# Where the written order of an MLP's instructions begins and ends, in a two-layer attention kernel on one core

## The chip, the core and the metric

The kernel runs on one core of a Trainium2 chip. Its engines are TensorE (PE in the profile, with PEld for its weight loads), VectorE (DVE), ScalarE (ACT), GpSimd (POOL) and SyncE (SP, which here only issues DMAs). The metric is device microseconds (us) of one execution; before the change the median of three runs is 2160.49 us (2158.95 to 2161.11).

## The reference

Two layers on 256 tokens of width 2048, all in float32. Layer 0 is stick-breaking attention with 16 heads, layer 1 a native sparse attention (compressed, selected and windowed branches with gates); after each comes an MLP. What matters here is the skeleton:

```
def sqrelu_mlp(h, w1, w2):
    return jnp.square(jax.nn.relu(h @ w1)) @ w2

for layer in range(2):
    h = h + attention(rms_norm(h, norm_g))
    h = h + sqrelu_mlp(rms_norm(h, mlp_norm_g[layer]), mlp_w1[layer], mlp_w2[layer])
```

w1 is 2048 x 8192, w2 is 8192 x 2048.

## The kernel before

**Chunks.** Every large product is done in chunks of a 2 x 128-row by 512-column block (512 KB) of weights. SP loads a chunk into a `raw` tile (five in rotation; in the MLPs three loads in eight go into `more`, three in rotation). ScalarE rounds it to `hi` (L143) and VectorE makes the rest `lo = raw - hi` (L145); both have four buffers in rotation. TensorE then multiplies high and low halves in three products. A tile in rotation is free again when its last reader is done: the `hi` buffer of a chunk, when the chunk's `hi` matmuls have ended.

**What lies between two large products.** The activations are kept transposed, in `xs` (high and low). When a 512-column block of h is complete (`add_h`, L387, or L385 without a factor), `next_x` takes its square sums on ScalarE (`ssq`, L350, tile `junk`), TensorE transposes it (`make_x`, L329, four transposes into a bank of `att`), and ScalarE (L334) and VectorE (L336) write `xs`. The generator `next_x` is put into a list, and `pump`, called twice in each chunk, lets it advance.

**The MLP.** w1 is taken in four quarters of hidden columns (`fg`), each in four parts of eight chunks (`T` chunks, `chunk1`, L207). Of w2's products some output blocks are done plainly (`N` chunks, `chunk2`, L174) and some with Strassen's scheme (`S` chunks, `chunk7`, L270), whose sums `add_S` adds to h (`sum7`: first `uv` on ScalarE, L294, then seven steps on VectorE, L295 to L299); `sum2` adds a plain block. In the last quarter the order is 24 `N` chunks for output blocks 0, 1 and 3, eight `S` chunks for block 2 among them, and behind the last `S` chunk six more `N` chunks. `done` starts `next_x` for a block (first MLP) or stores it (second).

**What sets the order.** Each engine runs its instructions in the order in which they stand in the program. In general a scheduler sets that order when the program is built. Inside `tc.manual_schedule(engines=...)` the instructions of the named engines keep the order in which the kernel's code issues them. In the kernel before, all steps of an MLP are inside such a block, for TensorE, VectorE, ScalarE and SP: from the first chunk of w1 on, with the `next_x` of the last output block that `pump` mixes in, to the end, where the first MLP's `next_x` for the next attention is mixed in likewise. `plan()` yields the steps; `put(after, j, ...)` places a step behind the j-th chunk of a list.

Of the kernel before, what the change touches and what calls it, by code (L numbers as in the profile page):

```python
# [16 lines left out]
T = 256  # L17
# [18 lines left out]
SK = 2 * ST + NCMP  # L36
GATES = 3 * NH
JUNK = 1
SLOPES = [2.0 ** (-8.0 * (i + 1) / NH) for i in range(NH)]


@with_exitstack
def hybrid_kernel(
# [15 lines left out]
    att = ctx.enter_context(tc.tile_pool(name="att", bufs=4, space=PSUM))  # L59
# [358 lines left out]
    def mlp(l, layer, junk, done, last=None):  # L418
        w1, w2 = mlp_w1[l], mlp_w2[l]
        ss = far(junk, KD * 4 * P, "ss").rearrange("p (a k i n) -> p a k i n", a=2, k=KD // 2, i=4)  # L420
        factor = junk.tile([P, 64], F32, name="factor", bufs=1)[:, :NT]
        NK, NF, NG, KB = KD // KC, D // NB, DFF // D, NB // P
        banks, part = {}, {}

        def factors():
            yield
            r = make_rstd(layer)
            nc.vector.tensor_tensor(factor, r, r, op=OP.mult)

        def chunk1(fg, fb, i):  # L430
            if i == 0:
                banks["T", fb] = [bank(acc, "acc") for _ in range(KB // 2)]
            chunk_T(banks["T", fb], w1, i * KC, fg * D + fb * NB, i == 0, i == NK - 1)

        def relu(fb):
            a = part["s", fb] = junk.tile([P, KB, T], F32, tag="sq", name="sq", bufs=1)
            for j in range(0, KB, 2):
                nc.scalar.activation(
                    a[:, j:j + 2, :], banks["T", fb][j // 2].rearrange("p (m t) -> p m t", m=2), AF.Relu
                )  # L440

        def square(fb):
            s = part["s", fb]
            nc.scalar.activation(s, s, AF.Square)

        def high(fb):
            k, s = fb * KB, part["s", fb]
            nc.scalar.activation(yhi[:, k:k + KB, :], s, AF.Copy)
            sv = s.rearrange("p (j kk) t -> p j kk t", kk=2)
            a1, a2 = [[sv[:, :, kk, t * P:(t + 1) * P] for kk in (1, 0)] for t in range(NT)]  # L450
            q = part["q", fb] = junk.tile([P, 2, 4, P], F32, tag="sums", name="sums", bufs=1)
            nc.vector.scalar_tensor_tensor(q[:, :, 0, :], a2[0], -1.0, a2[1], op0=OP.mult, op1=OP.subtract)
            nc.vector.tensor_tensor(q[:, :, 2, :], a1[0], a2[0], op=OP.subtract)
            nc.vector.tensor_tensor(q[:, :, 1, :], a2[1], q[:, :, 2, :], op=OP.subtract)
            nc.vector.tensor_tensor(q[:, :, 3, :], a1[1], q[:, :, 1, :], op=OP.subtract)

        def low(fb):
            k, s = fb * KB, part["s", fb]
            nc.scalar.activation(ss[:, 0, k // 2:k // 2 + 2], part["q", fb], AF.Copy)
            nc.vector.tensor_tensor(ylo[:, k:k + KB, :], s, yhi[:, k:k + KB, :].bitcast(F32), op=OP.subtract)  # L460

        def low7(fb):
            k = fb * KB
            o = ss[:, :, k // 2:k // 2 + 2]
            nc.vector.tensor_tensor(o[:, 1], part["q", fb], o[:, 0].bitcast(F32), op=OP.subtract)

        def chunk2(fg, nb, i, first, end, turn, by_token=False):
            if first:
                banks["N", nb] = [bank(acc, "acc") for _ in range(NT)]
            chunk_N(banks["N", nb], w2, fg * KD + i * KC, nb * NB, first, end, yhi, ylo, koff=fg * KD,  # L470
                    by_token=by_token, turn=turn)

        def chunk7(fg, nb, i, first, end):
            if first:
                banks["S", nb] = banks_S(att, "att")
            chunk_S(banks["S", nb][1], w2, fg * KD + i * KC, nb * NB, first, end, yhi, ylo, ss[:, 0], ss[:, 1],
                    koff=fg * KD)

        def sum2(nb):
            add_h(nb, banks["N", nb], factor)  # L480

        def sum7(nb):
            add_S(nb, *banks["S", nb], junk, factor)

        def plan():


            def merge(plain, after):
                for j, c in enumerate(plain):
                    yield c  # L490
                    yield from after.pop(j, ())
                assert not after

            def do(f, *args):
                return lambda: f(*args)

            def Ts(fg, fb):
                return [("T", fg, fb, i) for i in range(NK)]

            def Ns(fg, nb, ks=range(NK)):  # L500
                return [("N", fg, nb, i, i == ks[0], i == ks[-1]) for i in ks]

            def Ss(fg, nb, at, after, ks=range(NK)):
                for i, j in zip(ks, at):
                    after.setdefault(j, []).append(("S", fg, nb, i, i == ks[0], i == ks[-1]))

            def put(after, j, *fs):
                after.setdefault(j, []).extend(fs)

            def stages(after, j, fb, stash=False):  # L510
                if not stash:
                    put(after, j, do(relu, fb))
                put(after, j, do(square, fb))
                for i, f in enumerate((high, low, low7)):
                    put(after, j + 1 + i, do(f, fb))

            half = NK // 2
            for fg in range(NG):
                after = {}
                if fg == 0:  # L520
                    plain = sum([Ts(0, fb) for fb in range(NF)], [])
                    for fb in range(NF - 1):
                        stages(after, fb * NK + NK + 2, fb)
                else:
                    plain = sum([Ts(fg, fb) for fb in range(1, NF)], [])
                    put(after, 2, do(sum7, 2))
                    put(after, 3, do(sum2, 1))
                    Ss(fg - 1, 3, (3, 5, 7, 10, 13, 15, 18, 21), after)
                    stages(after, 8, 0, True)
                    stages(after, 13, 1)  # L530
                    stages(after, 18, 2)
                yield from merge(plain, after)
                after = {}
                if fg:
                    put(after, 1, do(sum7, 3))
                stages(after, 2, NF - 1)
                if fg < NG - 1:
                    plain = Ns(fg, 0) + Ts(fg + 1, 0) + Ns(fg, 1, range(half, NK))
                    Ss(fg, 1, (4, 5, 6, 7), after, range(half))
                    put(after, 10, do(sum7, 1))  # L540
                    put(after, 11, do(sum2, 0))
                    Ss(fg, 2, (12, 13, 14, 15, 16, 17, 18, 19), after)
                    put(after, 18, do(relu, 0))
                else:
                    plain = Ns(fg, 0) + Ns(fg, 1) + Ns(fg, 3)
                    put(after, 10, do(sum2, 0))
                    Ss(fg, 2, (4, 6, 8, 10, 11, 13, 15, 17), after)
                    put(after, 17, do(sum2, 1))
                    put(after, 18, do(sum7, 2), *[do(done, n, (att, "att")) for n in range(3)])
                    if last is None:  # L550
                        put(after, 23, do(sum2, 3), do(done, 3, (att, "att")))
                yield from merge(plain, after)

        spawn(factors(), 1)
        with tc.manual_schedule(engines={mybir.EngineType.PE, mybir.EngineType.DVE, mybir.EngineType.Activation,
                                         mybir.EngineType.SP}):
            steps = list(plan())
            for n, c in enumerate(steps):
                if callable(c):
                    c()  # L560
                    continue
                follower = next((d[0] for d in steps[n + 1:] if not callable(d)), None)
                if c[0] == "T":
                    chunk1(*c[1:])
                elif c[0] == "S":
                    chunk7(*c[1:])
                elif last is not None and c[1:3] == (NG - 1, 3):
                    fg, nb, i, first, end = c[1:]
                    chunk2(fg, nb, i, first, i == NK - 2, False, end)
                else:  # L570
                    chunk2(*c[1:], turn=follower in ("T", "S"))
            if last is not None:
                add_out(3, banks["N", 3], last, factor)

# [627 lines left out]
```

## Time and profile before

| | |
|---|---|
| median of three runs | 2160.49 us |
| the profiled execution's own time | 2155.24 us |
| its span, first to last instruction | 2153.5 us |
| mean granted TensorE clock | 0.998 |
| TensorE busy | 2134.2 us (99%) |
| VectorE, ScalarE, GpSimd busy | 1654.2, 1232.2, 45.5 us |
| DMA | 406.38 MB, mean 189 GB/s |

The page gives the busy time of each engine; a view of waits tells for whom an engine waited; the timeline lists the instructions of one engine in order of time (start, duration, engine, line, operation, tiles, count, and in brackets the idle time before it and who ended it). A view by windows gives for each stretch of time its length, the busy time of an engine, and the clock that TensorE was granted. On TensorE the first MLP goes from 391.8 to 1080.5 us of the span, the second from 1465.0 us to the end.

### The profile page before, as it was taken

The page shows a single profiled execution, that of the slowest core. Times are in us where ns is not written, and L with a number is a line of the kernel's source. Part 1 is how long each engine was busy: PE and PEld are TensorE (multiplying, and loading weights), DVE is VectorE, ACT ScalarE, POOL GpSimd, SP SyncE. Part 2 cuts the span into 40 slices and gives each one's busy share as a digit, 9 for nine tenths or more (in the row PEclk, how much of TensorE's full clock was granted, in tenths as well). Part 3 has the DMA queues.
Part 4 walks back from the last instruction along what each step waited for, and adds up shares of the span by engine and source line. Part 5 has one row for each costly group of instructions (what it writes and reads, how often), then busy time and mean ns, then how long its engine had stood idle before and what let it go on. Part 6 is the DMA issues. An engine that isn't in the chain of part 4 may idle for free. (4 is left out here: it accounts for less than half of the span.)

```text
span 2153.5 us, 37647 instructions
## 1 busy us (share of the span) xinstructions
PE 2134.2 (99%) x15110; PEld 1979.8 (92%) x15110; DVE 1654.2 (77%) x2269; ACT 1232.2 (57%) x1683; POOL 45.5 (2%) x78
## 2 busy tenths in 40 slices
PE   9999999999999999999999999999999999999999
PEld 9999988899999999999898888888999999999997
DVE  5556556468989989889687888764589889899896
ACT  6555665455565565565455666654555655655653
POOL 0000000000000000000000100000000000000000
PEclk9999999999999999999999999999999999999999
DMA  7655555566766666666477554455657666666663
GB/s 238 211 169 176 160 182 178 184 202 184 213 196 200 201 205 196 197 214 199 144 197 219 168 145 137 147 189 157 203 185 213 196 200 205 203 197 198 208 214 118
DMA packets 260407, 406.38 MB, mean 189 GB/s; under 512 B 13188, under 2 KB 91912, under 8 KB 260232
## 3 DMA queue, kind: packets, MB, share of 16 engines
q1 hardware_dynamic: 258984, 401.95, 60.6%
q8 instruction: 118, 1.93, 0.4%
q0 software_dynamic: 432, 1.57, 0.2%
q10 hardware_dynamic: 816, 0.46, 0.1%
q14 instruction: 57, 0.47, 0.1%
HBM read 401.83 MB, written 2.10 MB: 188 GB/s over the span
## 5 line engine op out<-in xcount | busy, mean ns | idle before, releaser
L145 DVE TENSOR_TENSOR lo<-raw,hi 128x1024 fp32r<-128x1024 f32 x486 | 590.1, 1221 | 210.8 <-ACT hi L143 201.5
L143 ACT ACTIVATE hi<-raw 128x1024 fp32r<-128x1024 f32 x486 | 509.8, 1054 | 291.5 <-PE acc L174 122.4
L207 PE MATMUL acc<-xs,hi 128*128 128x256 f32 x5360 | 667.3, 277 | 8.3 <-ACT hi L143 7.7
L207 PEld LDWEIGHTS acc<-xs,hi 128*128 128x128 f32 x5360 | 635.9, 188 | 10.2 <-ACT hi L143 8.8
L207 PE MATMUL acc<-xs,lo 128*128 128x256 f32 x2680 | 361.4, 278 | 0.0
L207 PEld LDWEIGHTS acc<-xs,lo 128*128 128x128 f32 x2680 | 331.4, 189 | 0.0
L174 PE MATMUL acc<-hi,yhi 128*128 128x512 f32 x732 | 287.1, 392 | 2.9 <-ACT hi L143 2.9
L174 PE MATMUL acc<-hi,ylo 128*128 128x512 f32 x732 | 285.6, 390 | 0.0
L143 ACT ACTIVATE hi<-ts 128x1024 fp32r<-128x1024 f32 x136 | 144.3, 1061 | 186.8 <-DVE ts L250 185.3
L174 PE MATMUL acc<-lo,yhi 128*128 128x512 f32 x732 | 198.5, 392 | 1.1 <-DVE lo L145 1.1
L145 DVE TENSOR_TENSOR lo<-more,hi 128x1024 fp32r<-128x1024 f32 x129 | 157.4, 1220 | 45.9 <-ACT hi L143 45.2
L145 DVE TENSOR_TENSOR lo<-ts,hi 128x1024 fp32r<-128x1024 f32 x136 | 166.4, 1223 | 23.9 <-ACT hi L143 22.8
L174 PE MATMUL acc<-hi,xs 128*128 128x512 f32 x704 | 177.8, 392 | 0.0
L174 PEld LDWEIGHTS acc<-hi,yhi 128*128 128x128 f32 x732 | 137.4, 188 | 29.4 <-ACT hi L143 3.3
L174 PEld LDWEIGHTS acc<-lo,yhi 128*128 128x128 f32 x732 | 136.5, 188 | 29.8 <-DVE lo L145 2.0
L174 PEld LDWEIGHTS acc<-hi,ylo 128*128 128x128 f32 x732 | 137.5, 188 | 26.0 <-DVE ylo L316 0.2
L143 ACT ACTIVATE hi<-more 128x1024 fp32r<-128x1024 f32 x129 | 135.7, 1052 | 36.3 <-PE acc L207 21.1
L174 PEld LDWEIGHTS acc<-hi,xs 128*128 128x128 f32 x704 | 130.1, 188 | 26.0
L248 ACT ACTIVATE shi<-raw 128x768 fp32r<-128x768 f32 x73 | 61.8, 846 | 103.3 <-PE att L270 103.3
L270 PE MATMUL att<-hi,ss 128*128 128x256 f32 x816 | 114.6, 276 | 0.0
L248 ACT ACTIVATE shi<-more 128x768 fp32r<-128x768 f32 x63 | 53.2, 844 | 97.0 <-PE att L270 97.0
L270 PEld LDWEIGHTS att<-hi,ss 128*128 128x128 f32 x816 | 102.6, 188 | 0.0
(256 smaller groups left out, 2627.5 us busy)
## 6 DMA issues: line engine op xcount, KB each, us to landing
raw<-in_mlp_w_dram SPq DMA_DIRECT2D x320, 512.0 KB, 4.1
more<-in_mlp_w_dram SPq DMA_DIRECT2D x192, 512.0 KB, 4.1
raw<-in_sb_w_qkv_dram SPq DMA_DIRECT2D x95, 512.0 KB, 4.1
raw<-in_nsa_w_in_dram SPq DMA_DIRECT2D x50, 512.0 KB, 3.9
raw<-in_sb_w_out_dram SPq DMA_DIRECT2D x32, 512.0 KB, 4.2
raw<-in_nsa_w_in_dram SPq DMA_DIRECT2D x64, 256.0 KB, 3.8
raw<-in_nsa_w_out_dram SPq DMA_DIRECT2D x32, 512.0 KB, 3.6
w1t<-in_nsa_cmp_w_dram SPq DMA_DIRECT2D x8, 512.0 KB, 4.2
```

Of the source, the lines that this page charges most:

```text
L143: nc.scalar.activation(hi, raw, AF.Copy)
L145: nc.vector.tensor_tensor(lo, raw, hi.bitcast(F32), op=OP.subtract)
L174: mm = lambda a, b, k, t, s, e: nc.tensor.matmul(ps[t], a[:, k, t * P:(t + 1) * P], b, start=s, stop=e)
L207: nc.tensor.matmul(o, w, x[:, k0 + kk, :], start=s, stop=e, skip_group_check=True)
L248: nc.scalar.activation(hi, flat[:, :3 * W], AF.Copy)
L270: nc.tensor.matmul(ps[i], a, w, start=s, stop=e, skip_group_check=True)
```

## The change

The block of the written order no longer holds the whole MLP. It is entered at step `("T", 0, 1, 0)`, the first chunk of the second part of w1's first quarter; the eight chunks before it are left to the scheduler. In the first MLP it is closed behind the last `S` chunk by a marker in the plan (`FREE`); what follows (the sums, the six last `N` chunks, the `next_x` of the next attention) is left to the scheduler. In the second MLP it holds to the end, but `sum2(1)` moves from behind chunk 17 to behind chunk 18, and `sum7(2)` with three `done` from 18 to 20.

```diff
+FREE = "the scheduler's order from here"
...
                     Ss(fg, 2, (4, 6, 8, 10, 11, 13, 15, 17), after)
-                    put(after, 17, do(sum2, 1))
-                    put(after, 18, do(sum7, 2), *[do(done, n, (att, "att")) for n in range(3)])
                     if last is None:
+                        put(after, 17, FREE, do(sum2, 1), do(sum7, 2), *[do(done, n, (att, "att")) for n in range(3)])
                         put(after, 23, do(sum2, 3), do(done, 3, (att, "att")))
+                    else:
+                        put(after, 18, do(sum2, 1))
+                        put(after, 20, do(sum7, 2), *[do(done, n, (att, "att")) for n in range(3)])
...
-        with tc.manual_schedule(engines={mybir.EngineType.PE, mybir.EngineType.DVE, mybir.EngineType.Activation,
-                                         mybir.EngineType.SP}):
-            steps = list(plan())
+        steps = list(plan())
+        with ExitStack() as order:
             for n, c in enumerate(steps):
-                if callable(c):
+                if c == ("T", 0, 1, 0):
+                    order.enter_context(tc.manual_schedule(engines={
+                        mybir.EngineType.PE, mybir.EngineType.DVE, mybir.EngineType.Activation, mybir.EngineType.SP
+                    }))
+                if c == FREE:
+                    order.close()
+                elif callable(c):
                     c()
...
```

What this makes of the program's order, at three places. The changed file is eight lines longer; its line 144 is line 143 of the kernel before.

ScalarE at the start of the first MLP, before. `hi_3921` is the split of the first chunk of w1; `junk` are the square sums of h; `hi_3994`, `hi_4099` and `hi_4159` are splits out of `more`:

```order
L143 ACTIVATE hi_3921<-raw_3919 128x1024
L350 ACTIVATE junk_3949,ssq_3520<-h_77 128x512
L350 ACTIVATE junk_3951,ssq_3520<-h_77 128x512
L143 ACTIVATE hi_3955<-raw_3953 128x1024
L334 ACTIVATE xs_78<-att_3983,gT_90 128x256 x2
L143 ACTIVATE hi_3994<-more_3992 128x1024
L334 ACTIVATE xs_78<-att_4022,gT_90 128x256 x2
L143 ACTIVATE hi_4033<-raw_4031 128x1024
```

The same place with the change (`hi_3919` is now the split of the first chunk):

```order
L144 ACTIVATE hi_3919<-raw_3917 128x1024
L144 ACTIVATE hi_3953<-raw_3951 128x1024
L144 ACTIVATE hi_3992<-more_3990 128x1024
L144 ACTIVATE hi_4031<-raw_4029 128x1024
L351 ACTIVATE junk_3947,ssq_3520<-h_77 128x512
L351 ACTIVATE junk_3949,ssq_3520<-h_77 128x512
L144 ACTIVATE hi_4061<-raw_4059 128x1024
L144 ACTIVATE hi_4097<-more_4095 128x1024
L335 ACTIVATE xs_78<-att_3981,gT_90 128x256 x2
L144 ACTIVATE hi_4127<-raw_4125 128x1024
L335 ACTIVATE xs_78<-att_4020,gT_90 128x256 x2
```

Three splits moved ahead of the square sums, and two more ahead of the first `xs`; the start of the second MLP moves in the same way. On TensorE nothing moves at these two places. On SP, the loads there with the change:

```order
L159 DMA raw<-in_sb_w_out_dram 128x2x512 x19
L159 DMA more<-in_mlp_w_dram 128x2x512
L159 DMA raw<-in_sb_w_out_dram 128x2x512
L159 DMA more<-in_mlp_w_dram 128x2x512
L159 DMA raw<-in_sb_w_out_dram 128x2x512
L159 DMA more<-in_mlp_w_dram 128x2x512
L159 DMA raw<-in_sb_w_out_dram 128x2x512 x11
L159 DMA raw<-in_mlp_w_dram 128x2x512 x7
```

Before, all 32 loads of the output projection's weights stood ahead of the MLP's first; now three loads into `more` stand ahead of 13, 12 and 11 of them.

ScalarE at the end of the first MLP, before, from the split of the last `S` chunk (`hi_11505`) on; `hi_11534` is the split of the first `N` chunk behind it, `uv` the first step of the Strassen sum:

```order
L143 ACTIVATE hi_11505<-ts_11497 128x1024
L143 ACTIVATE hi_11534<-more_11532 128x1024
L294 ACTIVATE uv_11550<-att_11005 128x256
L143 ACTIVATE hi_11561<-raw_11559 128x1024
L350 ACTIVATE junk_11578,ssq_11577<-h_77 128x512
L350 ACTIVATE junk_11580,ssq_11577<-h_77 128x512
L143 ACTIVATE hi_11584<-raw_11582 128x1024
L334 ACTIVATE xs_78<-att_11596,gT_90 128x256 x2
L334 ACTIVATE xs_78<-att_11609,gT_90 128x256 x2
L143 ACTIVATE hi_11620<-more_11618 128x1024
```

With the change:

```order
L144 ACTIVATE hi_11505<-ts_11497 128x1024
L144 ACTIVATE hi_11544<-more_11542 128x1024
L351 ACTIVATE junk_11619,ssq_11560<-h_77 128x512
L351 ACTIVATE junk_11621,ssq_11560<-h_77 128x512
L144 ACTIVATE hi_11567<-raw_11565 128x1024
L144 ACTIVATE hi_11603<-raw_11601 128x1024
L144 ACTIVATE hi_11625<-more_11623 128x1024
L295 ACTIVATE uv_11533<-att_11005 128x256
L144 ACTIVATE hi_11661<-raw_11659 128x1024
L351 ACTIVATE junk_11677,ssq_11560<-h_77 128x512
L144 ACTIVATE hi_11683<-more_11681 128x1024
L335 ACTIVATE xs_78<-att_11579,gT_90 128x256 x2
```

Square sums and three splits moved ahead of `uv`, two more splits ahead of the first `xs`. TensorE's transposes of this stretch stand one `N` chunk earlier, the last of them one chunk of the next projection earlier.

VectorE at the end of the second MLP, with the change (before, `lo_23370` and `lo_23388` stood, under other numbers, behind the last of the `h<-uv` additions, and the two `h<-acc` one row earlier):

```order
L146 TENSOR_TENSOR lo_23350<-raw_23346,hi_23348 128x1024
L388 SCALAR_TENSOR_TENSOR h_77<-acc_22950,factor_15730,h_77 128x512
L388 SCALAR_TENSOR_TENSOR h_77<-acc_22951,factor_15730,h_77 128x512
L146 TENSOR_TENSOR lo_23370<-more_23366,hi_23368 128x1024
L146 TENSOR_TENSOR lo_23388<-raw_23384,hi_23386 128x1024
L296 TENSOR_TENSOR uv_23402<-att_22824,uv_23402 128x256
L297 TENSOR_TENSOR uv_23402<-att_22823,uv_23402 128x256
```

The `lo` halves of two `N` chunks moved ahead of the Strassen sum.

More of the change, by code (lines that the diff above doesn't have):

```diff
@@ L552, in plan @@
                 yield from merge(plain, after)
         spawn(factors(), 1)
-        with tc.manual_schedule(engines={mybir.EngineType.PE, mybir.EngineType.DVE, mybir.EngineType.Activation,
-                                         mybir.EngineType.SP}):
-            steps = list(plan())
+        steps = list(plan())
+        with ExitStack() as order:
             for n, c in enumerate(steps):
-                if callable(c):
-                    c()
[L561 to L569, printed above, removed]
-                else:
-                    chunk2(*c[1:], turn=follower in ("T", "S"))
+                if c == ("T", 0, 1, 0):
[5 more added lines that the diff above has]
+                elif callable(c):
+                    c()
+                else:
+                    follower = next((d[0] for d in steps[n + 1:] if not callable(d) and d != FREE), None)
+                    if c[0] == "T":
+                        chunk1(*c[1:])
+                    elif c[0] == "S":
+                        chunk7(*c[1:])
+                    elif last is not None and c[1:3] == (NG - 1, 3):
+                        fg, nb, i, first, end = c[1:]
+                        chunk2(fg, nb, i, first, i == NK - 2, False, end)
+                    else:
+                        chunk2(*c[1:], turn=follower in ("T", "S"))
```

## The prediction

> **What bounds the kernel now.** The page's first part has TensorE busy for 2134.2 us of a span of 2153.5 us, so no edit off TensorE pays unless TensorE waits for it. I read next who TensorE waits for (line, releaser, total us, times, longest), over the whole span:
>
> ```profile
> PE acc L207 <- ACT hi L143: 7.7, 5, 1.9
> PE acc L174 <- ACT hi L143: 2.9, 2, 1.9
> PE acc L174 <- DVE lo L145: 1.1, 2, 0.6
> PE acc L207 <- ACT xs L334: 0.6, 1, 0.6
> ```
>
> The busy total hides more than these 12.3 us: a matmul at half clock counts as busy. So I cut the stretches where the waits lie (columns: from:to, length, TensorE busy and instructions, granted clock, share of the DMA engines, GB/s). The first, third and fifth are the start of the first MLP, its end with the seam to the next attention, and the start of the second MLP; the last is the end of the second MLP; the second and fourth are undisturbed pieces for comparison.
>
> ```profile
> 391.77:409.71 17.94, 14.19 (x105) 0.91 0.33 89
> 409.71:420.64 10.93, 10.93 (x97) 1.00 0.87 286
> 1057.04:1096.30 39.26, 35.24 (x229) 1.00 0.46 137
> 1465.02:1484.83 19.81, 15.87 (x106) 0.83 0.30 81
> 1484.83:1495.79 10.96, 10.96 (x97) 0.99 0.88 287
> 2134.98:2138.56 3.58, 3.00 (x13) 1.00 0.18 71
> ```
>
> What a chunk (24 matmuls of 256 columns, or 12 of 512) should take is read from the timeline of TensorE: from one chunk's start to the next 2.72 us (412.48 to 415.20; 380.60 to 383.32), and 3.20 us where a group of four transposes (L329) stands between (374.57 to 377.77), so 0.48 us a group.
>
> ```profile
> 374.57 0.48 PE L174 MATMUL acc<-hi,yhi 128*128 128x512 f32 x1
> 377.77 0.48 PE L174 MATMUL acc<-hi,yhi 128*128 128x512 f32 x1
> 380.60 0.39 PE L174 MATMUL acc<-hi,yhi 128*128 128x512 f32 x1
> 383.32 0.39 PE L174 MATMUL acc<-hi,yhi 128*128 128x512 f32 x1
> 412.48 1.98 PE L207 MATMUL acc<-xs,hi 128*128 128x256 f32 x16
> 415.20 1.98 PE L207 MATMUL acc<-xs,hi 128*128 128x256 f32 x16
> ```
>
> **Why TensorE waits at the start of an MLP.** ScalarE's timeline there:
>
> ```profile
> 382.61 1.06 ACT L143 ACTIVATE hi<-raw 128x1024 fp32r<-128x1024 f32 x1 [1.66 <-PE acc L174]
> 392.17 0.63 ACT L350 ACTIVATE junk<-h 128x512 f32<-128x512 f32 x1 [8.50 <-DVE h L385]
> 398.14 0.84 ACT L334 ACTIVATE xs<-att,gT 128x256 fp32r<-128x256 f32 x2 [3.54 <-PE att L329]
> 398.87 1.05 ACT L143 ACTIVATE hi<-more 128x1024 fp32r<-128x1024 f32 x1
> 403.46 0.84 ACT L334 ACTIVATE xs<-att,gT 128x256 fp32r<-128x256 f32 x2 [3.54 <-PE att L329]
> ```
>
> ScalarE works in order. The split of chunk 0 runs at 382.61; the next row in its queue is the square sum of h, which waits 8.50 us for the last addition to h; the split of chunk 2 (`hi<-more`) stands behind `xs`, which waits for transposes that TensorE does behind chunk 1. Nothing holds the split itself: its tile was filled long before, and its `hi` buffer (four in rotation) comes free with the last but one chunk of the output projection. So TensorE transposes, then idles 1.87 us for `xs` and the split behind it, twice (3.7 of the 7.7 us above). At 1465 the same happens, with 0.19 + 1.87 + 1.87 us.
>
> **The change there.** Outside the written order, ScalarE splits chunks 1, 2 and 3 ahead of the square sums, and 4 and 5 ahead of the first `xs`. TensorE's own order stays; only its input comes earlier. I walk it: the `hi` buffers come free as the last output chunks end their `hi` half, one each 2.72 us, so splits 1 to 3 run at about 385.4, 388.1 and 390.8 and are done before chunk 0 starts at 391.77; split 4 waits for chunk 0's `hi` half (about 393.6) and split 5 for chunk 1's (396.5), each two chunks ahead of its use; `xs` of the last two pairs comes at 398 to 402, and chunks 6 and 7, which read it, start near 409. VectorE's `lo` halves (1.2 us each) follow the same order. I find no wait left. The first stretch then costs 4 x 2.72 + 2 x 0.48 = 11.84 instead of 17.94: **6.1 us**; the third start 11.84 instead of 19.81: **8.0 us**.
>
> SP's queue is moved too: three loads of w1 into `more` go out some 13 loads of w_out earlier. The first of them waits for the last use of the attention's memory, TensorE's last product with `u` and `v`, and everything behind it on SP waits along. That product is at 331.24; SP's next load of w_out goes out at 331.79 anyway, held by a split. I cost it at nothing; what covers it are 8.5 us until the split of that load must have its data (344.41, less 4.1 us of landing), and, from the end of that split's two halves (344.41 + 1.06 + 1.2), another 8 us until TensorE comes to that chunk at 354.59.
>
> ```profile
> 354.59 0.48 PE L174 MATMUL acc<-hi,yhi 128*128 128x512 f32 x1
> ...
> 331.24 0.39 PE L736 MATMUL att<-u,v 128*128 128x128 f32 x2
> 331.79 4.49 SPq L158 DMA_DIRECT2D raw<-in_sb_w_out_dram  x2
> 344.41 1.06 ACT L143 ACTIVATE hi<-raw 128x1024 fp32r<-128x1024 f32 x1 [1.60 <-PE acc L174]
> more<-in_mlp_w_dram SPq DMA_DIRECT2D x192, 512.0 KB, 4.1
> ```
>
> **The end of the first MLP.** From 1057.04, when TensorE has left the last Strassen chunk, to 1096.30 stand six w2 chunks and five chunks of the next attention: 11 x 2.72 = 29.92, and eight groups of transposes (32 of them), 3.84: 33.76 in 39.26 us, so 5.5 us lost, in four waits.
>
> ```profile
> L329 PE MATMUL att<-ident,h 128*128 128x128 f32 x32 | 4.5, 273 | 0.0
> ...
> 1056.56 0.38 ACT L294 ACTIVATE uv<-att 128x256 f32<-128x256 f32 x1 [6.14 <-PE att L270]
> 1062.31 1.20 PE L174 MATMUL acc<-lo,yhi 128*128 128x512 f32 x4 [0.56 <-DVE lo L145]
> 1069.01 0.50 PE L174 MATMUL acc<-hi,yhi 128*128 128x512 f32 x1 [1.87 <-ACT hi L143]
> 1077.57 0.50 PE L174 MATMUL acc<-hi,yhi 128*128 128x512 f32 x1 [1.00 <-ACT hi L143]
> 1090.50 0.38 PE L207 MATMUL acc<-xs,hi 128*128 128x256 f32 x1 [0.59 <-ACT xs L334]
> ```
>
> `uv`, the first step of adding the Strassen result to h, waits 6.14 us on ScalarE, and the splits of the next w2 chunks stand behind it; later ones stand behind `xs` as above. In the new order three splits run ahead of `uv` and the next stand ahead of the first `xs`. One of the three waits for the Strassen chunk's own `hi` matmuls (about 1056.2), so `uv` ends near 1057.6, 0.7 us later; the transposes that need its bank now stand at about 1062.7, so this is covered by some 5 us. The transposes themselves move up by a w2 chunk, and the last group by one chunk of the next projection, so `xs` is ready (about 1085) when the chunk that reads it starts near 1084.3, pair by pair: the tightest place, worth 0 to 0.6 us (the wait of 0.59 above is the nearest row). I take 0.3: gain **5.2 us**.
>
> **The end of the second MLP.** Here the order stays written; the addition to h moves back one w2 chunk and the Strassen sum two, so the splits of w2 chunks 2 and 3 stand ahead of `uv` on both engines. The `lo` half that came late was queued behind the seven additions:
>
> ```profile
> 2136.25 1.22 DVE L145 TENSOR_TENSOR lo<-more,hi 128x1024 fp32r<-128x1024 f32 x1
> 2137.53 1.20 PE L174 MATMUL acc<-lo,yhi 128*128 128x512 f32 x4 [0.57 <-DVE lo L145]
> ```
>
> Chunk 2 takes 3.58 us instead of 2.72: **0.9 us**. The additions end at about 2136.3 as now, before the splits of chunk 4 are due near 2142, so nothing is passed on. Sum: 6.1 + 8.0 + 5.2 + 0.9 = 20.2 us. The profiled execution (2155.24, span 2153.5) would become 2135.0; the median of the three runs, 5.25 us above the profiled one, **2140.3**.
>
> **The part that hangs on the clock.** In stretches of 3.40 us:
>
> ```profile
> 403.40:406.80 3.40, 1.53 (x12) 0.93 0.28 104
> 406.80:410.20 3.40, 3.40 (x19) 0.56 0.75 201
> 1068.40:1071.80 3.40, 2.79 (x12) 1.00 0.01 2
> 1475.20:1478.60 3.40, 3.39 (x18) 0.57 0.54 154
> 1482.00:1485.40 3.40, 3.40 (x20) 0.57 0.75 219
> ```
>
> After a stretch with under half of it busy the clock is down to 0.56 for the next; after 2.79 busy it is not. Three such stretches lose about 3 x 0.44 x 3.4 = 4.5 us of the 20.2, and I count them as caused by the gaps. The Trainium skill ("TensorE: Matmul & The Clock Gate", section "HAM oscillation — how this bites in real kernels") has the rule that TensorE is throttled again by idle gaps of more than about 3.4 us; by it gaps of 1.87 us would not do this, the drops would have another cause and stay, and the sum would be 4.5 us less. The rows speak against that reading.
>
> **The rivals.**
> 1. The slow clock stays (some other cause): 20.2 - 4.5 = 15.7, time 2144.8. For it: no wait in the list is longer than 1.9 us. Against: each drop follows directly on the idle stretch, in both MLPs.
> 2. The end of the first MLP does not close: engines off the written order run into each other (square sums, `xs`, additions and splits are mixed differently on ScalarE and VectorE), and the loss of 5.2 us returns: 2145.5. For it: that place has four waits of three kinds and my walk leaves under 1 us in one spot.
> 3. TensorE waits at the MLP starts for something that is merely named after the split, such as the weights' arrival: then 14.1 of the 20.2 us stay away, 2154.4. Against: the wait's releaser is ScalarE, and the split that ends the first gap (398.87) starts as `xs` ends, with the `more` tile loaded some 20 us before.
> 4. Slower: the first early `more` load holds SP. The load of w_out behind it needs its place by 340.3; each us beyond that makes a split late, and after the further 8 us TensorE stands still, 1:1. To undo 20.2 us the hold must last 8.5 + 8 + 20 = 37 us; with 50 us it would be 2160.5 + 13 = 2173. The row at 331.24 says that the hold is nil, unless the attention's end moves, which nothing in the change moves.
>
> **How the numbers follow.** Forecast 0.75, rival 1 0.07, rival 2 0.12, rival 3 0.04, rival 4 0.02. The lower bound takes the gap of 5.25 us between the profiled execution and the median: if the timed runs lose three or four more stretches to the slow clock (1.5 us each), these go as well, 2140.3 - 6 = 2134. The upper bound holds rivals 1 and 2 with the runs' scatter of 2 us: 2148. A measurement tells 0.2% (4.3 us) from no change; all of the forecast and rivals 1 and 2 lie beyond it: faster 0.94; rival 3, 6.1 us faster, lies near the bound and its 0.04 I count as the same; slower 0.02.
>
> **What would show it.** Right: the four lines of waits above shrink to about 1 us together; the stretch from chunk 0 to chunk 4 of either MLP is about 11.9 us at clock 1.00; ScalarE's `hi` rows stand ahead of `junk<-h` with idle time put down to TensorE's `acc`; chunk 2 behind the last Strassen chunk of the second MLP takes 2.7. Wrong: a wait of TensorE for `lo` or `att` between 1057 and 1096, a clock under 1 without an idle stretch before it, or w_out splits that wait for DMA before 390.

## The result, and the profile after

The changed kernel takes 2136.55 us (median of four runs, 2136.23 to 2138.28) where the kernel before takes 2159.72 us beside it (2155.82 to 2161.11): a ratio of 0.9897, 95% interval 0.9880 to 0.9914, so 1.0% faster. The forecast was 2140.3 us, between 2134.0 and 2148.0. Span against span, the profiled execution after has 2134.5 us and the one before 2153.5: 19.0 us less, where the sum of the prediction had 20.2.

The prediction names two of its six stretches the wrong way round: the second and the *fifth* are the undisturbed pieces, and the *fourth* (from 1465.02) is the start of the second MLP. The terms themselves use the right rows.

Who TensorE waits for after the change, over the whole span (line, releaser, total us, times, longest; lines of the changed kernel are one higher, 8 higher in its later parts):

```profile
PE att L603 <- POOL ident masks.py:199: 1.6, 1, 1.6
PE att L906 <- DVE a L897: 1.1, 1, 1.1
PE acc L622 <- ACT hi L615: 1.0, 2, 0.8
PE att L924 <- DVE kc L919: 0.4, 1, 0.4
```

All four lines that the prediction rested on (`hi`, `lo`, `xs` of the weight chunks, 12.3 us) are gone. What is left is the start of the program and two places in the attention. The same pieces of work as before, cut from the changed kernel's trace (from:to, length, TensorE busy and instructions, granted clock, DMA share, GB/s): start of the first MLP from chunk 0 to chunk 4; eleven chunks behind the last Strassen chunk of the first MLP; the eight chunks that follow them; start of the second MLP; chunk 2 at the end of the second MLP.

```profile
391.72:403.65 11.93, 11.93 (x105) 1.00 0.64 179
1050.93:1084.95 34.02, 34.02 (x229) 1.00 0.51 146
1084.95:1107.56 22.61, 22.61 (x194) 1.00 0.63 174
1454.75:1466.75 12.00, 12.00 (x105) 1.00 0.66 182
2116.82:2119.54 2.72, 2.72 (x14) 1.00 0.00 0
```

The first, second, fourth and fifth were 17.94, 39.26, 19.81 and 3.58 us. They give 6.0 + 5.2 + 7.8 + 0.9 = 19.9 us. TensorE is busy in all of them from end to end, at full clock. The third is the surprise: eight chunks in 22.61 us are 2.83 us each, though nothing waits and the clock is 1.00. In the kernel before, eight chunks of that projection took 2.72 each:

```profile
1096.30:1118.06 21.76, 21.76 (x195) 1.00 0.65 181
```

Ten chunks run so after the change (1082.04 to 1110.83). The first of them lies in the second stretch already; the nine behind it take back 0.9 of the 19.9 us, which is the difference between the four places and the spans.

ScalarE's timeline at the start of the first MLP shows the mechanism at work:

```profile
385.28 1.06 ACT L144 ACTIVATE hi<-raw 128x1024 fp32r<-128x1024 f32 x1 [1.66 <-PE acc L175]
388.05 1.06 ACT L144 ACTIVATE hi<-more 128x1024 fp32r<-128x1024 f32 x1 [1.71 <-PE acc L175]
390.72 1.06 ACT L144 ACTIVATE hi<-raw 128x1024 fp32r<-128x1024 f32 x1 [1.61 <-PE acc L175]
392.12 0.63 ACT L351 ACTIVATE junk<-h 128x512 f32<-128x512 f32 x1 [0.35 <-DVE h L386]
...
396.58 1.06 ACT L144 ACTIVATE hi<-more 128x1024 fp32r<-128x1024 f32 x1 [1.66 <-PE acc L208]
397.94 0.84 ACT L335 ACTIVATE xs<-att,gT 128x256 fp32r<-128x256 f32 x2 [0.29 <-PE att L330]
```

Three splits stand ahead of the square sum `junk<-h`, at 385.3, 388.1 and 390.7 (the walk in the prediction had 385.4, 388.1 and 390.8). The square sum finds h nearly ready (0.35 us of waiting instead of 8.50), and `xs` comes behind split 5 instead of ahead of split 2.

### The profile page after: what moved, and what is told of

Same layout as the page of the kernel before. It is cut to its first block, busy times and chain, and to the rows that moved or that the text cites. A ratio compares the mean times of both kernels' runs of the same rounds, so it can differ in the third digit from the quotient of the medians.

```text
span 2134.5 us, 37649 instructions
## 1 busy us (share of the span) xinstructions
PE 2126.6 (100%) x15110; PEld 1974.6 (93%) x15110; DVE 1654.9 (78%) x2269; ACT 1235.0 (58%) x1683; POOL 45.0 (2%) x78
## 4 chain that ended last, share of the span: by engine, by line
PE 98%; DMA 0%; DVE 0%; issue 0%; ACT 0%; POOL 0%; SPq 0%; DVEq 0%; ACTq 0%
PE acc L208 43%; PE acc L175 34%; PE att L271 15%; PE att L175 1%; PE att L1032 1%; PE att L330 1%; PE att L743 0%; PE att L695 0%; PE att L970 0%; PE att L1026 0%; PE att L972 0%; PE att L971 0%; PE att L1024 0%; PE att L1025 0%; PE att L948 0%
```

## The experiments

**Each place by itself.** Theory: a place is worth what its own stretch loses, because TensorE is the only bound and has no slack elsewhere. Rivals: the waits at the starts are only named after the splits; the slow clock has a cause of its own; the end of the first MLP hangs on the starts.

First the two starts alone. The written order begins with the second quarter of w1, and is kept to the end in both MLPs, with the old places of the sums:

```
-                    if last is None:
-                        put(after, 17, FREE, do(sum2, 1), do(sum7, 2), ...)
-                        ...
+                    put(after, 17, do(sum2, 1))
+                    put(after, 18, do(sum7, 2), ...)
+                    if last is None:
+                        put(after, 23, do(sum2, 3), do(done, 3, (att, "att")))
```

> The changed kernel with its written order entered at the second quarter of w1 in both MLPs, but kept to the end of the first MLP as before, and with the old places of the Strassen sums; only the two starts are free. My theory (each place is worth what its own stretch loses): from chunk 0 to chunk 4 about 11.9 us instead of 17.9 (first MLP) and 12.0 instead of 19.8 (second), so 13.8 us less than before; the end of the first MLP keeps its 39.3 us and its four waits, chunk 2 at the end of the second its 3.6 us. Rival (the wait is only named after the split; what is late is the weights or SP): the starts keep 14 of their us and the time falls by under 2 us. A second rival (the slow clock has a cause of its own): the waits go, the clock stays at 0.9 and 0.83 in the two stretches, and the gain is 9.3 us.

Measured 2142.82 us (2141.68 to 2143.76) against 2156.21 beside it: 13.4 us less, ratio 0.9936 (0.9919 to 0.9952). Both stretches in its trace:

```profile
391.29:403.22 11.93, 11.93 (x106) 1.00 0.63 179
1460.98:1472.99 12.01, 12.01 (x105) 1.00 0.68 180
```

The theory holds at the starts, and the two rivals with 2 and 9.3 us fall. The span of the profiled execution is 11.9 us shorter than that of the kernel before, and not 13.8: a wait of 1.87 us at the end of the first MLP, which this kernel keeps, was followed by a stretch at half clock (1062.68 to 1066.09) that the profiled execution before did not have.

Then the end of the first MLP alone: the written order from the first step, left behind the last Strassen chunk.

```
-                if c == ("T", 0, 1, 0):
+                if n == 0:
                     order.enter_context(tc.manual_schedule(...))
```

> The written order from the first step of both MLPs as before, but left behind the last Strassen chunk of the first MLP as in the changed kernel; places of the Strassen sums in the second MLP as before. My theory: the stretch of eleven chunks behind the last Strassen chunk of the first MLP falls from 39.26 to about 34.0 us, so 5.2 us less; the two starts keep 17.9 and 19.8 us. Rival (the gain there hangs on the starts): under 1 us. Behind the stretch the changed kernel's projection ran ten chunks at 2.82 us instead of 2.72, 1.0 us in all: if the order behind the Strassen chunk itself sets that pace, it is here too and the gain is 4.2 us; if it is chance, 5.2.

Measured 2149.46 us (2147.55 to 2150.76): 6.8 us below the 2156.21, ratio 0.9965 (0.9952 to 0.9978). In its trace the eleven chunks take 34.01 us, as in the changed kernel, with no wait among them; the two starts keep their waits:

```profile
1055.09:1089.10 34.01, 34.01 (x229) 1.00 0.52 146
```

So the rival that the gain there needs the starts falls. The slow pace behind it is here too (2.05 us for 16 matmuls of the projection from 1089.10 on, instead of 1.98), but the order behind the Strassen chunk does not decide it alone. Three kernels that keep TensorE's old order there (the starts alone, above; the splits moved by hand and the gaps filled, below) show the ten slow chunks in their traces too; the kernel before and the one with only the end of the second MLP changed do not. With the slow pace 4.2 us were expected, and the median gave 2.5 more. Those three traces show what the other executions of the kernel before may lose here and the profiled one did not: about 1.0 us by the slow chunks, and 1.7 us by a stretch at half clock behind a wait of 1.87 us. The two parts give 13.39 + 6.75 = 20.1 us by the medians; the changed kernel, run again in the next set, 21.7.

The end of the second MLP alone, in the kernel before:

```
-                    put(after, 17, do(sum2, 1))
-                    put(after, 18, do(sum7, 2), ...)
+                    put(after, 17 + (last is not None), do(sum2, 1))
+                    put(after, 18 + 2 * (last is not None), do(sum7, 2), ...)
```

> The kernel before with only the two numbers at the end of the second MLP moved (the addition to h behind w2 chunk 2 instead of 1 there, the Strassen sum behind chunk 4 instead of 2). My theory: chunk 2 there takes 2.72 instead of 3.58 us and nothing else changes: 0.9 us less, within the scatter of the medians and so told by the profile. Rival (what is spared comes back at the additions of the last chunks): chunk 2 at 2.72, and a wait of 0.5 us or more later in the last 20 us.

The time says nothing (2158.22 us, 2150.97 to 2162.70, against 2157.99; ratio 0.9999, 0.9988 to 1.0009), and with a scatter of 12 us it could not. The trace does: chunk 2 takes 2.72 us, and TensorE waits for nothing from 2130 us to the end.

```profile
2136.54:2139.26 2.72, 2.72 (x13) 1.00 0.00 0
```

**Is it the queue of ScalarE, or SP?** Here nothing is left to the scheduler, and TensorE's and SP's orders are those of the kernel before. Only the splits of the first quarter of w1 are issued three chunks ahead:

```
         def chunk1(fg, fb, i):
+            src = w1
+            if (fg, fb) == (0, 0):
+                while len(ready) < min(i + 4, NK):
+                    ready.append(load_split(w1, len(ready) * KC, KC, 0, NB, o=(FAR, FAR)))
+                src = ready[i]
-            chunk_T(banks["T", fb], w1, ...)
+            chunk_T(banks["T", fb], src, ...)
```

> The kernel before with one thing moved by hand: in the first quarter of w1, in both MLPs, the splits of chunks 0 to 3 are issued ahead of chunk 0, and each later chunk's three chunks ahead. On ScalarE and VectorE splits stand ahead of square sums and of the new xs; TensorE's and SP's order stay as before, and nothing is left to the scheduler. My theory (the split stood behind xs and the square sum in the queue of ScalarE): the same gain as with the free starts, 13.8 us. Rival (the earlier loads of w1 on SP bring it, or the weights come late): under 2 us.

Measured 2144.40 us (2143.24 to 2145.76), ratio 0.9944 (0.9930 to 0.9959): 11.8 us less. The stretches are the same as with the free starts:

```profile
393.36:405.29 11.93, 11.93 (x106) 1.00 0.57 160
1463.39:1475.39 12.00, 12.00 (x105) 1.00 0.59 159
```

So the place of the splits in ScalarE's and VectorE's queues is the cause, and SP's earlier loads of w1 bring nothing and cost nothing at these places. The 1.6 us by which its median is above the one with free starts do not come from there: in its profile the first long chunk of the program starts at 12.16 us instead of 10.09. The kernel before, whose orders up to there are the same, has 10.57, and a late start shows in a profile of another kernel below, so it belongs to the execution.

**Do the gaps cause the slow clock?** The kernel before, with its waits filled by work that nobody reads:

```
             make_x(kp, g0, pool)
+            if nb == 3 and layer != "nsa":
+                fill = bank(att, "att")
+                for _ in range(14):
+                    nc.tensor.transpose(fill[:, :P], ident, ident)
```

> The kernel before with 14 transposes of the identity into a spare bank behind each of the two last groups of transposes at the start of either MLP: TensorE's two waits of 1.87 us are filled with about 1.65 us of work that nobody reads; all engines' orders are else as before, so chunk 2 and chunk 3 start when they did. My theory (the idle stretch takes the clock down to 0.56): the clock stays at 1.00 in both stretches and 4.5 us go, 1.5 in the first MLP and 3.0 in the second, though the splits come as late as before. Rival (the slow clock has a cause of its own, such as the heat or the traffic of the weights): the clock stays at 0.91 and 0.83 and the time within 0.5 us.

Measured 2153.31 us (2151.04 to 2154.71), ratio 0.9988 (0.9979 to 0.9998): 2.9 us less than before, though every split comes as late as before. In the profile:

```profile
391.66:408.02 16.36, 15.67 (x133) 1.00 0.25 70
1467.67:1484.33 16.66, 15.78 (x133) 1.00 0.26 68
```

The clock is 1.00 in both, and 17.94 - 16.36 = 1.6 and 19.81 - 16.66 = 3.1 us are gone, 4.7 together. So the gaps do cause the slow clock, and rival 1 of the prediction falls; the waits by themselves are the other 9.1 of the 13.8 us. The span of the whole profiled execution, though, is only 0.5 us shorter than before (2153.0 against 2153.5). At the end of the first MLP, where nothing was filled, a gap was followed by half clock, and the projection behind it ran at the slow pace (the last row: eight chunks, 21.76 us before):

```profile
1064.46:1067.87 3.41, 1.54 (x10) 1.00 0.26 89
1067.87:1071.28 3.41, 3.41 (x10) 0.50 0.00 0
1097.01:1119.62 22.61, 22.61 (x194) 1.00 0.62 173
```

With longer waits for `xs` there and in the next attention this took back 4.2 us. The median shows 2.9 us and not 4.7, and the run with the end of the first MLP alone had gaps of 1.87 us at the start of the first MLP and no drop at all. So a gap of this length does not always cost the clock. Cutting the traces to the edges of the slow stretches shows why. Before, around the second gap of the first MLP and both of the second:

```profile
402.93:406.34 3.41, 1.54 (x14) 1.00 0.37 133
406.34:409.75 3.41, 3.41 (x19) 0.50 0.61 159
1471.29:1474.70 3.41, 1.54 (x14) 1.00 0.39 134
1474.70:1478.12 3.42, 3.42 (x19) 0.50 0.54 153
1478.12:1481.53 3.41, 1.54 (x13) 1.00 0.00 0
1481.53:1484.94 3.41, 3.41 (x18) 0.50 0.61 170
```

Each slow stretch has the same length, 3.41 us, at exactly half clock, and their edges lie on one grid: from 406.34 to 1474.70 are 313 times 3.4133 us (the remainder of an edge by 3.4133 is 0.16 here). Ahead of each stands a window of that grid with 1.54 us busy: a gap of 1.87 us that lies wholly inside it. With the end of the first MLP alone the grid lay otherwise (remainder 2.08). Both gaps of the first MLP were split between windows; in the second MLP, the last two rows, one lay wholly inside:

```profile
398.02:401.43 3.41, 1.77 (x15) 1.00 0.18 70
401.43:404.85 3.42, 1.66 (x15) 1.00 0.52 153
404.85:408.26 3.41, 3.30 (x29) 1.00 0.28 44
1469.80:1473.21 3.41, 1.54 (x14) 1.00 0.51 145
1473.21:1476.62 3.41, 3.41 (x19) 0.50 0.43 101
```

After 1.77 and 1.66 us busy the clock stays; after 1.54 it halves. The threshold lies between 45% and 49% of the window. The fourteen traces of this case agree: 14 windows of the grid with 1.54 us busy, half clock behind each of them, and no drop from full to half clock behind a window with 1.66 us or more. A gap of 1.87 us at a chance place lies wholly inside a window in (3.41 - 1.87) / 3.41 = 45% of the cases. The Trainium skill ("TensorE: Matmul & The Clock Gate", section "Part 1: The HAM clock gate") tells of a free-running window of 3413 ns; the grid agrees to the digit. The rule of the Trainium skill on gaps over 3.4 us ("TensorE: Matmul & The Clock Gate", section "HAM oscillation — how this bites in real kernels") does not hold here: 1.87 us were enough.

**Gaps of several lengths.** This theory was put to the test with the end of the first MLP freed and 0, 2, 4 and 14 transposes in each of the four gaps (the kernel is that of the run with this end alone, and the transposes are added as in the last edit, with another number).

> The kernel with only the end of the first MLP freed, again, beside the two that follow: its four gaps of 1.87 us at the starts are as before. Theory W (read from six traces so far: the clock is judged over windows of 3.41 us on a grid that begins anew with each execution; after a window of which 1.54 us or less is busy the next one runs at half clock and costs 1.7 us, after 1.66 us busy it does not): a gap of 1.87 us costs a window only where it lies wholly inside one, in 45% of the cases, so 0 to 4 windows, mostly 1 to 3; median about 2149, runs from 2146 to 2153. Rival (each gap of some length costs the clock, wherever it lies): every run the same, within 1 us.

> The same with two transposes of the identity (0.24 us of work that nobody reads) in each of the four gaps, so that 1.6 us of each stay idle. Theory W: no window can be less than 1.75 us busy, so no half clock at all: clock 1.00 in both starts, the time at its best value, 2146 with at most 2 us of scatter from the start of the program, 3 us below the run without the transposes, although chunks 2 and 3 start no earlier. Rival (a gap of 1.6 us still costs the clock): the clock falls below 1 in the starts in the same share of cases, and the median stays near 2149.

> The same with 14 transposes in each gap, so that 0.35 us stay idle. Theory W: the same as with two, within 0.5 us. Rival (what counts is how much is idle): clearly less than with two transposes, by 1 us or more.

> As the kernel with two transposes in each gap, but with four (0.48 us), so that about 1.4 us of each gap stay idle. With two, the clock stayed at 1.00, yet 58 chunks ran at 2.83 us instead of 2.72, 6 us in all. Theory W and P together (no half clock, since no window is under 1.9 us busy; and the slow pace follows on short matmuls whose number between two chunks is not a multiple of four, as 2, 3 and 6 were): clock 1.00, 2.72 us a chunk behind the gaps, time 2146.1 as with 14. W alone (the pace is set by something else, such as the length of the wait): clock 1.00, the slow pace, 2152. Neither (1.4 us idle still cost the clock): runs between 2146 and 2153.

| transposes in each gap | idle left | time (us) | runs | mean clock |
|---|---|---|---|---|
| 0 | 1.87 | 2151.67 | 2150.54 to 2153.98 | 0.997 to 0.999 |
| 2 | 1.66 | 2152.21 | 2152.15 to 2152.92 | 1.000 |
| 4 | 1.44 | 2146.69 | 2145.99 to 2151.82 | 1.000 |
| 14 | 0.35 | 2146.09 | 2146.03 to 2147.77 | 1.000 |

The first row is the kernel with the end of the first MLP alone, run a second time: 2151.67 us here, 2149.46 above.

For the clock the theory holds: with 1.66 us idle or less it is 1.000 in all eighteen runs, with 1.87 in none of eight. For the time it fails. Without transposes the median is 2.7 us above the expected 2149, and with two all eight runs are 6 us above the expected 2146. The trace with two transposes, first the start of the first MLP, then the 27 chunks behind it:

```profile
391.63:408.17 16.54, 13.23 (x110) 1.00 0.27 69
408.17:484.49 76.32, 76.32 (x651) 1.00 0.68 207
```

The same two pieces with four transposes:

```profile
391.26:407.61 16.35, 13.48 (x113) 1.00 0.27 69
407.61:481.05 73.44, 73.44 (x650) 1.00 0.68 215
```

Nothing waits, the clock is full, and the chunks take 76.32 / 27 = 2.83 us instead of 2.72: 2.9 us in each MLP. It is the slow pace of the projection again, and it lasts until other matmuls break the row. The three runs with four transposes at 2145.99 to 2146.69 go with theory W and P. The other two, at 2149.29 and 2151.82 and clock 1.000, look like one and two slow quarters, but they have no profile. So a multiple of four does not keep the pace away for certain, and theory P falls as a rule.

**What sets the slow pace.** In the changed kernel the ten slow chunks begin behind two transposes of rstd. One or two more of the identity were put behind them:

```
                     pb = bcast_rows(rstd)
+                    for _ in range(2):
+                        nc.tensor.transpose(pb[:, T:T + P], ident, ident)
```

> The changed kernel with one more transpose of the identity (0.12 us) behind the two transposes of rstd in the projection that follows the first MLP, where from 1082.04 on ten chunks took 2.82 us instead of 2.72. Theory A (the pace is a state of the stream of matmuls that a pair of short ones set, and another number of them sets otherwise): the ten chunks take 2.72 and the time falls by 0.9 us. Theory B (the pace comes from what else runs there, such as the transfers or the places in memory): still 2.82, and the time is 0.1 us up.

> As the kernel with one more transpose, but with two (0.24 us). Theory A with the number's parity as what decides: the pace stays at 2.82 here and is 2.72 with one. Theory A without parity: 2.72 in both. Theory B: 2.82 in both, the time 0.2 us up.

> The changed kernel itself, beside the other runs of this set and the same runs of the kernel before. If the places add up (starts 13.4 and end of the first MLP 6.7 us by the medians, 0.9 at the end of the second by the profile), it is 21 us faster than before, about 2135; if the gains overlap, 17 or less. My theory on the projection behind the first MLP: the slow pace (2.82 us a chunk for ten chunks) comes back at the same place in a new profile, because it follows from the order of the instructions; rival: it is chance, and this profile has 2.72.

The changed kernel came out at 2136.27 us (2136.13 to 2136.49; 0.9900, 0.9884 to 0.9915, against 2157.99), with the ten chunks as slow as the first time. The five profiles of kernels that free the end of the first MLP alone (without transposes at the starts twice, with 2, 4 and 14) have them too, so in the new order the pace there is no chance. With one more transpose 2136.51 (2136.38 to 2138.15), still slow; with two more 2135.71 (2135.54 to 2137.29), and the pace is gone. TensorE in the changed kernel, run again:

```profile
1081.63 0.38 PE L379 MATMUL att<-ident,rstd 128*128 128x128 f32 x2
1081.77 2.13 PE L208 MATMUL acc<-xs,hi 128*128 128x256 f32 x16
1083.73 1.10 PE L208 MATMUL acc<-xs,lo 128*128 128x256 f32 x8
1084.67 2.05 PE L208 MATMUL acc<-xs,hi 128*128 128x256 f32 x16
```

and with two more transposes:

```profile
1083.50 0.38 PE L379 MATMUL att<-ident,rstd 128*128 128x128 f32 x2
1083.71 0.38 PE L1085 MATMUL att<-ident 128*128 128x128 f32 x2
1083.85 2.09 PE L208 MATMUL acc<-xs,hi 128*128 128x256 f32 x16
1085.77 1.07 PE L208 MATMUL acc<-xs,lo 128*128 128x256 f32 x8
1086.68 1.98 PE L208 MATMUL acc<-xs,hi 128*128 128x256 f32 x16
```

The other engines' orders, the transfers with them, are the same in both, so theory B falls, as far as one profile with two more transposes can tell. The pace is a state of TensorE's stream that a few short matmuls can start or end. The order of the matmuls is not all that sets it, since in the old order this projection ran fast in two traces and slow in three. Its cause is open: two and three transposes left it slow and four made it fast here, six with a wait behind them made it slow in the gaps, eighteen once slow and once fast (in the profile with 14 in each gap chunk 2 has 2.15 and chunk 3 has 2.08 us for its 16 matmuls), eight mostly fast. The run with two more transposes is the fastest version of this study, 0.6 us below the changed kernel by the medians; two of its five runs are above all of the changed kernel's in that set, so the times alone do not tell the two apart. In its profiled execution, one of the two, the first chunk of the program starts at 12.15 us instead of 10.29, which hides the gain there.

## Why the prediction was right, and where it was not

- **Start of the first MLP, 6.1 us; of the second, 8.0.** Right: 6.0 and 7.8 in the changed kernel, and the same with the free starts alone and with the splits moved by hand. The 0.1 and 0.2 us that are missing are the first chunk (2.85 instead of 2.72) in the first MLP, and two chunks at the slow pace in the second (1454.75 to 1460.76).
- **SP costs nothing.** Right: the stretches are equal to 0.01 us with SP's order moved and not moved. The load of w_out behind the first early load of w1 goes out at 331.96 us, where it went out at 331.79 before. Rivals 3 and 4 fall.
- **End of the first MLP, 5.2 us.** Right: 5.24, and 39.26 - 34.01 = 5.25 alone. The reading "5.5 us lost, in four waits" is not right, though: the four waits add up to 4.02 us, and the other 1.5 us lie in time in which TensorE counts as busy (35.24 us before, 34.02 after, for 229 instructions each). Rows of matmuls overlap in the timeline, but the last one before a wait stands alone to its end, so a wait costs more than its own length; that this makes the difference of 1.2 us is read from the rows and was not tested. The tight place is no wait at all. The 0.26 us above the 33.76 of the working, for which I had put 0.3 us of waiting, are something else: the two transposes of rstd (1081.90 to 1082.04), which the working left out, and the slow pace of the last chunk (1082.04 to 1084.95, 2.91 us). Rival 2 falls.
- **End of the second MLP, 0.9 us.** Right: 0.86, alone too, and nothing is passed on.
- **The part that hangs on the clock, 4.5 us.** Right as a cause, 4.7 us in the profiled execution. Too coarse as a rule: "under half of a stretch busy" is right only on the chip's own grid of windows, so each gap costs its 1.6 us with a chance of something under one half. The profiled execution lost three windows.
- **The sum, 20.2 against 19.0 us.** Two steps are off. The places bring 0.3 less, as above. And the sum ends at the places: it takes for granted that the chunks between them keep their 2.72 us. Nine of them did not, 0.9 us. In the new order the slow row begins behind the transposes of rstd; why the profiled execution before was spared it is open, since three traces with the old order have it too.
- **From the sum to the median, 2140.3 against 2136.55.** This is the step that was furthest off. I carried the 5.25 us between the profiled execution before and its median over to the kernel after, and gave their going away the lower bound only. After the change that difference is 0.02 us (2136.53 profiled, 2136.55 median). That the forecast still came within 3.8 us is in part luck: the 2135.0 of the working for the profiled execution was 1.5 us too low, and the carried 5.25 us too high. The difference is part of what the gaps cost. Without gaps there is no slow window that falls by chance: the kernel before scatters from 2152.25 to 2164.06 over all sets, the one with four gaps left at the starts from 2147.55 to 2153.98, the changed kernel from 2136.13 to 2138.28. Shown is that filling the gaps at the starts takes 2.9 us off the median and narrows the range of the runs from 5.6 to 3.7 us; three traces show that the gaps at the end of the first MLP can cost half clock as well. Half clock is not all of the scatter: among the 17 runs of the kernel before beside the second runs of the changed kernel, those with a mean clock of 0.998 take from 2154.46 to 2160.66 us, and the rounding of that clock leaves room for 2.2 us of it. That the rest of the 5.25 us is the slow pace behind gaps is argued, from the runs with two and four transposes and the three traces; none of the longer executions of the kernel before was profiled.

## What to carry to other kernels

Where the engine that bounds a kernel waits by turns for a split, a gain or a sum, look at which instruction stands *in front* of the late one in its queue: moving splits ahead of square sums and of `xs` that wait was worth 13.8 us at two places here, and nothing had to be computed faster. Price a gap on TensorE as its length plus a chance of half a window of clock, and do not carry the scatter of the old kernel over to the new one when the change takes away what scatters. A busy TensorE at full clock is not yet a TensorE at full pace: compare the time from chunk to chunk as well.

## What the runs showed of the hardware

- The clock is judged over windows of 3.41 us on a grid that begins at another place in each execution. Where TensorE was busy for 1.54 us of one, the next ran at half clock (14 of 14 windows, fourteen traces); 1.66 us were enough to keep it. Transposes of the identity count as busy: with only two of them in each gap of 1.87 us no run lost the clock.
- The same 24 matmuls of 128x256 take 2.72 or 2.83 us, at full clock and without a wait, in rows of up to 27 chunks (2.9 us). Short matmuls between two chunks can switch between the two, but one order of matmuls showed both; by which rule, these runs do not tell.
